# Moving five modulation rows into the up loop, pausing ahead of another, and widening the last batch of the down projection

## The chip, the cores and the metric

The kernel runs on one core of one Trainium2 chip. The metric is the device time of one execution in microseconds (us); lower is better. Engines are named as the profile names them: PE (matmul), PEld (its weight loads), DVE (vector), ACT (activation), POOL (GpSimd), SP (which only issues transfers here).

## The reference

One layer of a diffusion backbone runs over 512 sample tokens and 128 context tokens, all with model width 1024. Its modulation vector is `silu(cvec) @ w_ada + b_ada`, 6144 wide for each of two inputs (`c` and `c_ctx`); split six ways it gives two shifts, two scales and two gains:

```python
mod = jax.nn.silu(cvec) @ lw['w_ada'] + lw['b_ada']
sh1, sc1, g1, sh2, sc2, g2 = jnp.split(mod, 6, axis=-1)
h = rmsnorm(x, lw['norm1_g']) * (1.0 + sc1) + sh1
...                                    # token mixers, gates, w_o
x = x + g1 * mix
h = rmsnorm(x, lw['norm2_g']) * (1.0 + sc2) + sh2
x = x + g2 * conv_ffn(h, lw['w_up'], lw['ffn_conv_w'], lw['ffn_conv_b'], lw['w_down'])
```

`conv_ffn` is an up projection to 2 x 2816 columns, a three-tap convolution over tokens, `silu(g) * a`, and a down projection back to 1024. After the layer both token groups get a final RMS norm with `final_norm_g`. Neighbourhood attention is one of the four mixers.

## The kernel before, in words

**Number format.** Every large product is done three times, as high x high, high x low and low x high parts of float32; the part called "high" is made by a copy on ACT, the part called "low" by a subtraction on DVE or by an accumulating transfer that POOL issues. So each weight block that PE uses costs ACT and DVE work ahead of it ("preparing operands").

**Order.** The program is written out by hand in the order of PE. A small planner (`now`, `tick`, `start`, `step`, L89 to L122) advances a clock by the PE time of each matmul group; side jobs are Python generators that yield how long they want to wait, and they are written into the program when they fall due. A scheduler then orders each engine's instructions by when it believes their inputs to be ready. An instruction wrapped in `keep_in_program_order` (short: `keep_`, `sync` for transfers of SP, `ovec`/`oact`/`opool` inside the up loop) is pinned behind the instruction written last on its engine. Each engine then runs its queue strictly in order: one that waits holds up all behind it.

**Modulation rows.** The 6144 outputs are 48 "rows" of 128 columns. Rows 0 to 15 are done by PE at the start. The others are done on DVE: a 512 KB block of transposed weights is loaded (`H`, `X0`, `A` or `G`), and two `scalar_tensor_tensor` instructions (L285, one per input; the two inputs after silu stand in `S0`) multiply and sum it; a short instruction then writes the result, `modulate` (L231 or L234) for shifts and scales, `gain_col` (L291) for gains. Before the change `ada_cols` (L240) does rows 16 to 41 as a side job while the mixers run, each row yielding 1.4 between its parts and 2.2 ahead of the next; rows 42 to 47 are made inside the down projection by `col_make`, at the units that `COLS` names. Rows 40 to 47 are the gain g2, needed only at the outputs of the down projection, where `gain_rows(1)` (unit 26) and `gain_load` (unit 27) turn them into a broadcast tile in `S0`.

**Attention.** `attn` (L728) is another side job. Its steps for a pair of heads and a block of columns are s1 (scores on PE, sum at L848, maximum at L850, exponential on ACT at L851), s2 (reciprocal L857, scaling L858, transposes on PE at L861, a copy out) and s3 (values on PE at L878). It yields, times 1.1, 4.2 after the first s1, then in each turn 1.5 and 0.6 ahead of s2 and 3.2 behind it.

**Up loop.** `up_pair(p_, r)` (L1614) runs for p_ = 0 to 22. One pair is seven products of 12 matmuls (84 matmuls; a Strassen-like scheme with operands `A`, `B`, `C` and results added in PSUM). In each pair DVE subtracts and adds partial results, applies convolution taps (`taps`), and prepares the next pair's weights (`up_al`, `up_sums`, `up_bl`); ACT does copies, `centre` and silu (`gate`). All of it is pinned.

**Down projection.** 42 units, seven phases of six (`PHASES`, `DOWN`, L1807); a unit is two k steps (the sixth one), and has 12 or 18 matmuls of 512 columns. `ahead` issues the weight loads up to five units and prepares operands up to three units ahead. A unit named in `JOIN` holds its matmuls for the next one: in the last phase units 3, 4 and 5 run as one batch of five k steps, token tile by token tile (t = 0, 1, then 4 in two halves of 256 columns). Behind each token tile stand `half_two` and its parts: `gained` (L1960) and `added` (L1964) on DVE, a square on ACT (L2028), `half_join` (L2045), the root on POOL (`down_root`, L2048), the scaling (`down_scale` on ACT, `down_gain` at L2063 on DVE) and the store. Units named in `LATER` carry finished pieces of earlier phases; `final_gains` multiplies five half tiles by the final norm's weights on POOL and stores tiles 2 and 3.

Of the kernel before, what the change touches and what calls it, by code (L numbers as in the profile page):

```python
# [15 lines left out]

P = 128
HY = 5
AE = (("fb", 1), 0.5, 0.5, 42)
COLWAIT = {}  # L20
HD = [4, 5, 2.1, 7, 2.2, 1.4, 1.5, 5, 2.0, 2, 11]
NPAIR = 22
NK = NPAIR // 2
# [27 lines left out]
D = 1024  # L51
# [19 lines left out]
def tile_step(ctx: ExitStack, tc: tile.TileContext, a: dict, outs: list, dbg=None):  # L71
# [216 lines left out]
        return ar, steps()  # L288

    def gain_col(f, ar):  # L290
        vec.tensor_scalar(gcol[:, f // 8 // 5, :, f % 8], ar, p1[:, C_BADA + f:C_BADA + f + 1], None, ALU.add)  # L291

    def col_home(f):

# [1319 lines left out]
    def up_pair(p_, r):  # L1614


        n, q, o = p_ + 1, p_ - 1, p_ - 2
        inner, nx = p_ < NPAIR, n < NPAIR
        if p_ == 0:
            up_u2(p_)  # L1620
            up_back(1, "C", unit(1, 2), 5, 5, True)
            operand3()
# [10 lines left out]
        if nx and n >= BRIDGE:  # L1633
            up_ah(n, r[n][0])
            up_al(n, r[n][0])
        if inner and p_ >= BRIDGE:
            up_start(p_)
            first_sum(p_)
# [89 lines left out]
    def up_all(_):  # L1728
        fx["x"] = {1: (hh[0][:, 0], hh[0][:, 1]), 2: (hh[0][:, 2], hh[0][:, 3])}
        up_back(2, "A", unit(2, 0), 0, 4)  # L1730
        up_back(3, "A", unit(3, 0), 1, 4)
        up_back(0, "B", unit(0, 1), 2, 5)
        up_back(1, "B", unit(1, 1), 4, 5)
        drain(lambda: "n2_2" in R)
        for p_ in range(BRIDGE):
            up_start(p_)
            if p_ == 1:
                drain(lambda: "n2_3" in R)
                operands(0, 192)
# [12 lines left out]
        col_open()  # L1752

    units.append((lambda: None, lambda pr: None, up_all))


# [18 lines left out]
    def x_load(tag, part=None):  # L1775
# [11 lines left out]
        else:  # L1787
# [2 lines left out]
                xr[h, c] = region(tag, [P, 10, 256])  # L1790
            ks = slice(0, 10) if part is None else slice(5 * part, 5 * part + 5)
            sync(xr[h, c][:, ks], actx[h, c][:, ks])
            if part == 1:
                x_tail(h, c)

    def x_tail(h, c):
# [64 lines left out]
    hold = []  # L1861

    LAST = range(AE[3], 48)
    cols = {}

    def col_open():
        cols["c"] = region("S0", [P, 2, D])
        cf = cols["c"].rearrange("p v c -> p (v c)")
        sync(cf, a["cc"].rearrange("v c -> (v c)").partition_broadcast(P))
        keep_(act(cf, cf, AF.Silu))  # L1870
        for f in LAST[0:2]:
            col_load(f)

    def col_load(f):
        if f in LAST:
            cols[f] = region("HG"[f % 2], [P, D])
            sync(cols[f], a["w_adt"][f - 16])

    def col_make(f):
# [4 lines left out]
            pass  # L1884
        gain_col(f, ar[0])

    COLS = dict(zip((23, 21, 19, 9, 6, 3), range(47, 39, -1)))
    G2 = 27

    def down_start(u):  # L1890
        ph, j = DOWN[u]
        if u == 0:
# [5 lines left out]
        for tag, part in {0: (("A", 0), ("B", 0)), 2: (("A", 1), ("B", 1)), 6: (("D", 0),), 8: (("D", 1),),  # L1898
                          10: (("F", None),)}.get(u, ()):
            x_load(tag, part)  # L1900
        if u == 12:
            x2[2:4] = [x2r("X1")[:, 0:1024], x2r("X1")[:, 1024:2048]]
        if u - 2 in COLS:
            col_load(COLS[u - 2] + 2)
        if u in COLS:
            col_make(COLS[u])
        if u == G2 - 1:
# [16 lines left out]
    def down_tile(u, ws):  # L1924
# [9 lines left out]
        for t in (0, 1, 4) if hp is not None else (0, 1):  # L1934
            halved = p_ == 3 and t == 4 and end
            for ci, (c0, c1) in enumerate(((0, 256), (256, 512)) if halved else ((0, 512),)):
# [76 lines left out]
    def out_22(t):  # L2013
        joined(1, t + 2, acc["b2"][t], acc["u3"][t], ALU.subtract)

    LATER = {(5, 1): (lambda: out_22(0),), (5, 3): (lambda: out_22(1),), (5, 5): (lambda: out_11(0),),
             (6, 1): (lambda: out_11(1),), (6, 2): (lambda: out_11(4),), (6, 3): (final_gains,)}

    def half_two(nh, t, c0, c1, ps):
        xs = x2[t][:, nh * 512 + c0:nh * 512 + c1]  # L2020
        q1, q2 = (st3[:, i + t:i + t + 1] for i in (8, 16))
        keep_(gained(nh, t, c0, c1, ps))
        if t == 4 and c0 == 0:
            half_join(1, 8)
            down_root(1)
        keep_(added(nh, t, c0, c1))
        if c0 == 0:
            keep_(act(prods[t], xs, AF.Square, accum_out=q1))  # L2028
        if t == 1:
            down_store(nh, 0)  # L2030
        elif t < 4:
            half_join(t, 8)
            down_root(t)
        elif c0 > 0:
            half_join(t, 8)
            down_scale(nh, 1)
            keep_(vec.scalar_tensor_tensor(prods[t], xs, 1.0, xs, ALU.mult, ALU.mult, accum_out=q2))
            half_join(t, 16)
            down_root(t)
            down_gain(nh, 1)  # L2040
            down_store(nh, t)

    def half_join(t, i):
# [367 lines left out]
```

## Time and profile before

| | us |
|---|---|
| median of 3 runs | 1016.45 (1016.23 to 1018.08) |
| profiled execution, its time | 1015.32 |
| profiled execution, span of its instructions | 1013.2 |
| PE busy in it | 993.9 |
| DVE busy | 823.8 |
| ACT busy | 559.4 |
| mean granted PE clock | 0.996 |

The span is counted from the first to the last instruction of the profiled execution. In a timeline row the first number is the start in us from the span's start, the second the duration, then engine, line, operation, output and inputs, shape, count; in brackets the idle time of that engine just before it and what ended it. In a window row each engine has its busy time and, in brackets, its instruction count; then the granted PE clock as a share of full speed, the busy share of the transfer engines, and GB/s. "issue" is time with no wait that the profile shows. A line number can be that of a helper: L151 is the pinned form used in the up loop.

### The profile page before, as it was taken

Reading aid. Unit: us, or ns where it says so; the run is one execution under the profiler, and the core shown is the slowest. Engines: PE = TensorE matmul, PEld = TensorE weight load, DVE = VectorE, ACT = ScalarE, POOL = GpSimd, SP = SyncE. Lnnn points to the kernel's source line nnn. Section 1 sums busy time; section 2 is a strip of 40 time slices with the busy share of each in tenths; the row PEclk is TensorE's granted clock in tenths of the full one; section 3 lists DMA queues with packets and bytes.
Section 4 is the critical chain, followed back from the end, with each engine's and each line's share of the span. In section 5 each row is a group of like instructions: output and inputs, shape, how many; then the busy total and the mean of one; then the engine's idle time right before and its main releaser. Section 6 shows DMA issues by size and latency. Waiting matters only on the chain. (4 is left out here: it accounts for less than half of the span.)

```text
span 1013.2 us, 18951 instructions
## 1 busy us (share of the span) xinstructions
PE 993.9 (98%) x7503; PEld 941.4 (93%) x7503; DVE 823.8 (81%) x1381; ACT 559.4 (55%) x983; POOL 168.6 (17%) x223
## 2 busy tenths in 40 slices
PE   8999999997999999999999999999999999999996
PEld 6899999997999999999998899999999999888885
DVE  6778899867775667677778778998888887999897
ACT  6642343343464445444445376777777777756563
POOL 1000020322220122241010021222222222100013
PEclk9999999999999999999999999999999999999999
DMA  9875344596576399799249774766555666996462
GB/s 355 327 255 162 104 148 126 146 265 198 130 216 242 120 276 184 271 281 209 94 145 338 306 267 139 198 169 151 152 151 151 156 155 186 378 353 234 158 247 104
DMA packets 70010, 208.93 MB, mean 206 GB/s; under 512 B 9633, under 2 KB 24769, under 8 KB 67233
## 3 DMA queue, kind: packets, MB, share of 16 engines
q1 hardware_dynamic: 43536, 148.60, 41.2%
q0 software_dynamic: 26384, 59.12, 25.5%
q8 instruction: 59, 0.97, 0.4%
q14 instruction: 31, 0.25, 0.1%
HBM read 165.99 MB, written 48.51 MB: 212 GB/s over the span
## 5 line engine op out<-in xcount | busy, mean ns | idle before, releaser
L375 PE MATMUL g<-XH,w 128*128 128x320 f32 x704 | 171.7, 318 | 0.1
L375 PEld LDWEIGHTS g<-XH,w 128*128 128x128 f32 x704 | 121.2, 189 | 2.7 <-issue 1.0
L375 PE MATMUL g<-XL,w 128*128 128x320 f32 x352 | 109.0, 310 | 0.0
L375 PEld LDWEIGHTS g<-XL,w 128*128 128x128 f32 x352 | 66.6, 189 | 0.0
L1943 PE MATMUL m<-w,XH 128*128 128x512 f32 x246 | 58.6, 390 | 0.0
L1943 PEld LDWEIGHTS m<-w,XH 128*128 128x128 f32 x246 | 46.1, 188 | 9.7
L1152 PE MATMUL m<-XH,w 128*128 128x320 f32 x224 | 52.5, 309 | 0.0
L151 POOL DMA_DIRECT2D wsum<-in_w_dn_dram x36 | 36.5, 1154 | 53.0 <-issue 41.7
L151 ACT ACTIVATE w<-raw 128x1024 fp32r<-128x1024 f32 (+3 forms) x46 | 38.5, 852 | 2.3 <-DMA raw<-in_w_in_dram 1.1
L151 DVE SCALAR_TENSOR_TENSOR X<-MG,p2t,X 128x641 f32<-128x641 f32 x44 | 38.9, 884 | 1.1 <-ACT X L151 0.2
L151 DVE SCALAR_TENSOR_TENSOR X<-X,p2t,X 128x641 f32<-128x641 f32 x44 | 38.9, 884 | 1.0
L1512 PE MATMUL g<-XL,w 128*128 128x320 f32 x240 | 38.7, 310 | 0.0
L1152 PEld LDWEIGHTS m<-XH,w 128*128 128x128 f32 x224 | 38.3, 188 | 0.0
L1512 PE MATMUL g<-XL,C 128*128 128x320 f32 x240 | 38.3, 309 | 0.0
L1512 PEld LDWEIGHTS g<-XL,w 128*128 128x128 f32 x240 | 36.0, 188 | 0.6 <-ACT MG L151 0.3
L1512 PEld LDWEIGHTS g<-XL,C 128*128 128x128 f32 x240 | 36.0, 188 | 0.0
L1152 PE MATMUL m<-XL,w 128*128 128x320 f32 x112 | 34.6, 309 | 0.0
L151 ACT ACTIVATE ga<-m,cst 128x320 f32<-128x320 f32 x27 | 14.3, 528 | 36.6 <-PE m L1152 36.6
L151 DVE TENSOR_TENSOR w<-raw,w 128x1024 fp32r<-128x1024 f32 (+2 forms) x36 | 30.6, 871 | 2.5 <-ACT w L151 2.5
L151 ACT ACTIVATE X<-g 128x320 f32<-128x320 f32 x30 | 13.1, 437 | 34.6 <-PE g L1512 34.5
L1858 DVE TENSOR_TENSOR w<-raw,w 128x1024 fp32r<-128x1024 f32 (+1 forms) x26 | 30.1, 1156 | 2.5 <-ACT w L1854 2.5
L151 DVE TENSOR_TENSOR gb<-g,gb 128x640 f32<-128x640 f32 x12 | 9.9, 825 | 26.3 <-PE g L1165 25.4
(582 smaller groups left out, 2929.8 us busy)
## 6 DMA issues: line engine op xcount, KB each, us to landing
wsum<-in_w_dn_dram POOLq DMA_DIRECT2D x30, 512.0 KB, 11.7
raw<-in_w_up_dram SPq DMA_DIRECT2D x30, 512.0 KB, 5.5
raw<-in_w_gp_dram SPq DMA_DIRECT2D x21, 640.0 KB, 6.6
raw<-in_w_in_dram SPq DMA_DIRECT2D x19, 512.0 KB, 4.5
H<-in_w_adt_dram SPq DMA_DIRECT2D x16, 512.0 KB, 4.5
raw<-wsum SPq DMA_DIRECT2D x12, 512.0 KB, 5.3
actx<-X POOLq DMA_DIRECT2D x22, 256.0 KB, 4.4
wsum<-wsum POOLq DMA_DIRECT2D x10, 512.0 KB, 11.1
```

What stands on the lines that cost most here:

```text
L151: r = f(*args, **kw)
L375: mm(o, w[:, h, k0 + k, :], r(k)[:, s], start=(k == 0 and i == 0), stop=(k == kt - 1 and i == 2))
L1152: mm(o, w[:, k, :], x[:, k, :], start=(first and k == 0 and j == 0), stop=(k == 3 and j == 2), skip_group_check=True)
L1512: z = mm(o, w[:, k, :], x[:, k, :], start=(first and k == 0 and j == 0), stop=(k == 3 and j == 2), skip_group_check=True)
L1858: vec.tensor_tensor(w[:, 1, 0:n], raw, w[:, 0, 0:n].bitcast(F32), ALU.subtract)
L1943: mm(ps, s[t // 4][:, hx, k, o:o + P], w[:, hw, k, c0:c1], start=first, stop=i == 2 and bi == len(batch) - 1 and k == len(ks) - 1, skip_gr ...
```

## The change

Four things are edited together.

1. `ada_cols` does rows 16 to 39 only, and yields 8 ahead of row 39 (`AE`, `COLWAIT`).
2. Rows 40 to 44 are made in the up loop by the new `up_row`: pairs 6, 9, 12, 15 and 18 write a row's first product, the pair after each its second product, the gain column and the load of the next row. The two inputs are loaded and row 40's weights with them at pair 4 (`col_open`), and their silu is written at pair 6. Only rows 45, 46 and 47 stay in the down projection, at the same units as before (19, 21, 23); rows 46 and 47 are loaded two units ahead.
3. Loads in the down projection come later: `D` at units 9 and 11 (before 6 and 8), `F` at 13 (10), `X1` at 16 (12), the tail for `B` at unit 5 (2).
4. The last batch of the last phase has units 2 to 5, seven k steps instead of five. With it, the subtraction for the context tile moves from unit 2 to unit 1, `final_gains` from unit 3 to unit 5, and the token tiles close differently: tile 0 is scaled and stored right behind its own root, tile 1's root follows its own square, and tile 1 is scaled and stored whole between the two halves of tile 4.

```diff
-AE = (("fb", 1), 0.5, 0.5, 42)
-COLWAIT = {}
+AE = (("fb", 1), 0.5, 0.5, 40)
+COLWAIT = {39: 8}
...
+        if p_ == BRIDGE:
+            col_open()
...
         if nx and n >= BRIDGE:
             up_ah(n, r[n][0])
             up_al(n, r[n][0])
+            up_row(p_)
...
-            if part == 1:
+            if part == 1 and tag != "B":
                 x_tail(h, c)
...
-    JOIN = {(4, 4), (5, 0), (6, 3), (6, 4)}
+    JOIN = {(4, 4), (5, 0), (6, 2), (6, 3), (6, 4)}
...
+    UPROWS = dict(zip((6, 9, 12, 15, 18), LAST))
     cols = {}
+
+    def up_row(p_):
+        if p_ in UPROWS:
+            f = UPROWS[p_]
+            if f == LAST[0]:
+                cf = cols["c"].rearrange("p v c -> p (v c)")
+                keep_(act(cf, cf, AF.Silu))
+            cols["job"] = (f,) + col_products(f, cols.pop(f), cols["c"])
+        if "job" in cols:
+            f, ar, steps = cols["job"]
+            if next(steps) == 1:
+                keep_(gain_col(f, ar))
+                del cols["job"]
+                if f + 1 in LAST:
+                    col_load(f + 1)
...
-        keep_(act(cf, cf, AF.Silu))
-        for f in LAST[0:2]:
-            col_load(f)
+        col_load(LAST[0])
...
-            cols[f] = region("HG"[f % 2], [P, D])
+            cols[f] = region("G" if f == 46 else "H", [P, D])
...
-    COLS = dict(zip((23, 21, 19, 9, 6, 3), range(47, 39, -1)))
+    COLS = dict(zip((23, 21, 19), range(47, 44, -1)))
...
-        if p_ == 3 and j == 2:
+        if p_ == 3 and j == 1:
...
-             (6, 1): (lambda: out_11(1),), (6, 2): (lambda: out_11(4),), (6, 3): (final_gains,)}
+             (6, 1): (lambda: out_11(1),), (6, 2): (lambda: out_11(4),), (6, 5): (final_gains,)}
...
         keep_(gained(nh, t, c0, c1, ps))
-        if t == 4 and c0 == 0:
-            half_join(1, 8)
-            down_root(1)
         keep_(added(nh, t, c0, c1))
         if c0 == 0:
             keep_(act(prods[t], xs, AF.Square, accum_out=q1))
-        if t == 1:
-            down_store(nh, 0)
-        elif t < 4:
+        elif t == 4:
+            half_join(t, 8)
+        if t < 4:
             half_join(t, 8)
             down_root(t)
-        elif c0 > 0:
-            half_join(t, 8)
-            down_scale(nh, 1)
+            if t == 0:
+                down_store(nh, t)
+        elif c0 == 0:
+            down_store(nh, 1)
+        else:
             keep_(vec.scalar_tensor_tensor(prods[t], xs, 1.0, xs, ALU.mult, ALU.mult, accum_out=q2))
             half_join(t, 16)
             down_root(t)
-            down_gain(nh, 1)
             down_store(nh, t)
```

More of the change, by code (lines that the diff above doesn't have):

```diff
@@ L290, in gain_col @@
     def gain_col(f, ar):
-        vec.tensor_scalar(gcol[:, f // 8 // 5, :, f % 8], ar, p1[:, C_BADA + f:C_BADA + f + 1], None, ALU.add)
+        return vec.tensor_scalar(gcol[:, f // 8 // 5, :, f % 8], ar, p1[:, C_BADA + f:C_BADA + f + 1], None, ALU.add)
     def col_home(f):
@@ L1751, in up_all @@
         keep(NPAIR - 1)
-        col_open()
     units.append((lambda: None, lambda pr: None, up_all))
@@ L1897, in down_start @@
             acc["c1"], acc["u2"], acc["cp"] = [r[:, 0], r[:, 1]], [r[:, 2], r[:, 3]], r[:, 4]
-        for tag, part in {0: (("A", 0), ("B", 0)), 2: (("A", 1), ("B", 1)), 6: (("D", 0),), 8: (("D", 1),),
-                          10: (("F", None),)}.get(u, ()):
+        for tag, part in {0: (("A", 0), ("B", 0)), 2: (("A", 1), ("B", 1)), 9: (("D", 0),), 11: (("D", 1),),
+                          13: (("F", None),)}.get(u, ()):
             x_load(tag, part)
-        if u == 12:
+        if u == 5:
+            x_tail(1, 1)
+        if u == 16:
             x2[2:4] = [x2r("X1")[:, 0:1024], x2r("X1")[:, 1024:2048]]
-        if u - 2 in COLS:
-            col_load(COLS[u - 2] + 2)
+        if u + 2 in COLS and COLS[u + 2] > 45:
+            col_load(COLS[u + 2])
         if u in COLS:
```

## The prediction, made before the result was known

> **What bounds the kernel now.** I read the page's busy times and slices first, then the windows, then the one long wait of PE, then the end.
>
> ```profile
> span 1013.2 us, 18951 instructions
> ...
> PE 993.9 (98%) x7503; PEld 941.4 (93%) x7503; DVE 823.8 (81%) x1381; ACT 559.4 (55%) x983; POOL 168.6 (17%) x223
> ...
> PE   8999999997999999999999999999999999999996
> ```
>
> PE is busy 993.9 of 1013.2 us, so at most 19.3 us can be won without removing matmuls. The windows show where they lie:
>
> ```profile
> 225.00:250.00 25.00, 19.27 (x144) 17.61 (x143) 16.70 (x42) 9.14 (x21) 5.18 (x7) 0.93 0.72 229
> ...
> 725.00:750.00 25.00, 25.00 (x173) 25.00 (x172) 22.20 (x34) 17.88 (x31) 6.70 (x10) 1.00 0.60 154
> ...
> 900.00:925.00 25.00, 25.00 (x112) 20.69 (x111) 25.00 (x44) 13.66 (x21) 0.00 (x0) 1.00 0.91 337
> ...
> 1000.00:1025.00 25.00, 4.87 (x36) 4.47 (x34) 8.06 (x19) 3.91 (x9) 2.26 (x3) 0.86 0.26 103
> ```
>
> The reader is to see two holes that this change can touch: 25.00 - 19.27 = 5.73 us in the attention stage, and the end, where PE stops 4.87 us into the last window and 8.3 us of other work follow. In the up loop (725 to 750) and the down projection (900 to 925) PE is full. There DVE work moved away gains nothing by itself, and DVE work added costs nothing until a PE input is late.
>
> **The hole.** These are rows of DVE, PE, SP and ACT around it.
>
> ```profile
> 232.53 1.23 DVE L285 SCALAR_TENSOR_TENSOR junk<-A,S 128x1024 bf16<-128x1024 f32 x1 [7.56 <-DMA A<-in_w_adt_dram]
> ...
> 233.88 0.75 DVE L858 TENSOR_SCALAR X<-X,ast 128x384 f32<-128x384 f32 x2
> ```
> ```profile
> 234.44 1.51 PE L861 MATMUL m<-cst,X 128*128 128x128 f32 x6 [5.73 <-DVE X L858]
> ```
> ```profile
> 221.75 1.96 SPq L251 DMA_DIRECT2D A<-in_w_adt_dram  x1
> ```
> ```profile
> 225.53 0.19 ACT L851 ACTIVATION_READ_ACCUMULATOR X<-X,ast 128x1 f32 x1
> ```
> ```profile
> 234.00:236.00 2.00, 1.56 (x7) 1.59 (x8) 2.00 (x6) 0.00 (x0) 0.83 (x2) 0.50 0.04 15
> 236.00:238.00 2.00, 2.00 (x11) 2.00 (x11) 2.00 (x5) 1.95 (x5) 0.58 (x1) 0.71 0.00 0
> 238.00:240.00 2.00, 2.00 (x20) 1.81 (x20) 2.00 (x8) 0.68 (x2) 0.89 (x1) 1.00 0.66 162
> ```
>
> The L285 here is row 39's first product: it is the odd row in `A`, and after it only rows 40 and 41 follow. Its weights, issued at 221.75, landed at 232.5. DVE stood in front of it for 7.56 us with the softmax scaling (L858) queued behind, although the exponentials were done at 225.72. PE needed L858's output at 234.44 - 5.73 = 228.71. So the chain is: a late transfer, DVE's order, PE. The hole has a second cost, the clock behind it: 1.56 us at 0.50 and 2.00 us at 0.71 lose 0.78 + 0.58 = 1.36 us. Together 7.09 us.
>
> The Trainium skill ("TensorE: Matmul & The Clock Gate", Part 1) says that an idle window of about 3.4 us halves the PE clock, and that about 3.4 us of sustained work restores it. The trace agrees (5.73 us idle, then 0.50, then full by 238). An estimate from that page's figures alone would put the clock's share at up to 1.7 us and the hole at 7.4 instead of 7.09.
>
> **The change part by part.**
>
> *Pause ahead of row 39.* The product is due 8 later. By the planner's yields it was due 1.4 + 2.2 = 3.6 behind row 38's second product, just ahead of the second s1; now it is due 11.6 behind it. Row 38's second product is written at about the first s1, so s3 and the third s1, due 1.1 x (4.2 + 1.5 + 0.6 + 3.2) = 10.45 behind that, come first, and the product is pinned behind their DVE work. That work cannot start before about 228.71 + 3.5 = 232.2 and takes about two L848 and two L850, so the product is reached at 234 or later, when its weights have landed even at the old 232.5. L858 can then run at 225.8, two us ahead of need. Gain 5.73 + 1.36 = 7.09. Bounds: nothing gained if the transfer slips as far again, all 7.09 if it lands by 234; I take 7.09, since rows 40 and 41 no longer load behind it. Row 39's own result must be there for the last of four evacuations in this row, which drains until row 39 is done:
>
> ```profile
> L436 DVE TENSOR_TENSOR MG<-g,MG x4: 810/816/824, 245.1 to 278.2; 128x640 f32<-128x640 f32 x4
> ```
>
> At 278.2 - 7.1 = 271 against a row 39 finished near 240 it costs nothing.
>
> *Five rows in the up loop.* Prices, and one pair of the loop (DVE, then PE, then ACT):
>
> ```profile
> L285 DVE SCALAR_TENSOR_TENSOR H<-H,S x16: 1207/1218/1300, 64.7 to 942.1; 128x1024 f32<-128x1024 f32 x16
> L285 DVE DVE_READ_ACCUMULATOR H<-H,S x16: 73/82/85, 65.8 to 943.3; 128x1 f32 x16
> ```
> ```profile
> L291 DVE TENSOR_SCALAR gcol<-ar,cst x16: 210/222/228, 67.0 to 951.3; 128x2 f32<-128x2 f32 x16
> ```
> ```profile
> L1870 ACT ACTIVATE S<-S x1: 1904/1904/1904, 878.0 to 878.0; 128x2048 f32<-128x2048 f32 x1
> ```
> ```profile
> 719.44 1.23 DVE L151 TENSOR_TENSOR w<-raw,w 128x1024 fp32r<-128x1024 f32 x1 [0.35 <-ACT w L151]
> 721.61 0.49 DVE L151 TENSOR_TENSOR MG<-m,s 128x320 f32<-128x320 f32 x1 [0.95 <-PE m L1512]
> ...
> 727.01 0.48 DVE L151 TENSOR_TENSOR X<-g,X 128x320 f32<-128x320 f32 x1
> ```
> ```profile
> 717.82 1.92 PE L1512 MATMUL g<-XH,MG 128*128 128x320 f32 x12
> ...
> 723.10 1.92 PE L1512 MATMUL g<-A,E 128*128 128x320 f32 x12
> ...
> 730.14 1.92 PE L1512 MATMUL g<-XH,w 128*128 128x320 f32 x12
> ```
> ```profile
> 719.78 0.44 ACT L151 ACTIVATE s<-g 128x320 f32<-128x320 f32 x1 [0.38 <-PE g L1512]
> ```
>
> Ten products of 1.22 + 0.08 are 13.0 us and five gain columns 1.1: 14.1 us of DVE over pairs 6 to 19. A pair lasts 730.14 - 717.82 = 12.32 us and DVE idles 0.35 + 0.95 = 1.30 in it, 14 x 1.30 = 18.2 in all. The product is written between the weight subtraction (719.44) and the sum (721.61), exactly in the 0.95 wait. The first product overruns it by 0.35, the second with its gain column by 0.57; the backlog stays under 1 us, and the third pair clears it. What is late next is DVE's subtraction at 727.01, which frees the bank that PE writes from 730.14: 730.14 - 727.49 = 2.65 us of slack, more than the backlog. The silu (1.90, pair 6 only) delays ACT's copy from 719.78 + 0.44 = 720.22 to about 722.1; PE's product that overwrites its source starts at 723.10. Cost on PE: 0, the cover being these 2.65 and 1.0 us; if it were gone, all 14.1 + 1.9 would be the other end. The load of the next row stands on SP behind the second product and ahead of a later pair's weights; an SP that waits 1 us there delays loads whose buffers come free later anyway: 0.
>
> *Rows out of the down projection.* 3 x (2 x 1.30 + 0.22) = 8.5 us less DVE work around 885 to 908, and the silu. PE is full there: 0. *Later loads of D, F, X1, rows 46 and 47:* 0 if they land in time. The nearest row for one that does not is the 5.73 above; I keep 0, since three row loads and that of the inputs leave the same stretch of SP's queue.
>
> *The last batch.* PE, DVE and POOL at the end:
>
> ```profile
> 990.24 2.88 PE L1943 MATMUL m<-MG,XH 128*128 128x512 f32 x12
> ...
> 994.32 1.52 PE L1943 MATMUL m<-A,XH 128*128 128x512 f32 x6
> ...
> 1003.63 1.24 PE L1943 MATMUL m<-w,MG 128*128 128x256 f32 x9
> ```
> ```profile
> 992.67 0.68 DVE L1858 TENSOR_TENSOR w<-raw,w 128x512 fp32r<-128x512 f32 x1
> ...
> 999.59 0.68 DVE L1984 TENSOR_TENSOR y<-m,XL 128x512 f32<-128x512 f32 x1
> ...
> 1001.03 0.69 DVE L1964 TENSOR_TENSOR X<-X,dt 128x512 f32<-128x512 f32 x1
> 1002.58 0.16 DVE L2045 SCALAR_TENSOR_TENSOR st<-st 128x1 f32<-128x1 f32 x1 [0.85 <-ACT dt L2028]
> ...
> 1004.71 0.74 DVE L2063 SCALAR_TENSOR_TENSOR X<-X,st,F 128x512 f32<-128x512 f32 x1
> ...
> 1006.16 0.42 DVE L1960 TENSOR_TENSOR dt<-m,S 128x256 f32<-128x256 f32 x1
> ...
> 1008.80 0.75 DVE L2063 SCALAR_TENSOR_TENSOR G<-G,st,F 128x512 f32<-128x512 f32 x1 [0.44 <-POOL st L2048]
> ```
> ```profile
> 1002.81 0.55 POOL L2048 TENSOR_TENSOR st<-st,neghalf 128x1 f32<-128x1 f32 x1 [5.74 <-DVE st L2045]
> ...
> 1007.78 0.99 POOL L2048 TENSOR_TENSOR st<-st,neghalf 128x1 f32<-128x1 f32 x1 [1.13 <-DVE st L2045]
> ```
>
> A 512-wide matmul takes 2.72/12 = 0.227 us (990.24 to 992.96 in steps of 12). Tile 0 was finished at 994.32 + 15 x 0.227 = 997.7, and will be at 990.24 + 21 x 0.227 = 995.0. But DVE took it up only at 999.59: it is late, not PE, and stays so at the very end (the last half's sum runs at 1006.16, PE ended at 1004.87). The work ahead of 999.59 is the same after the change, so the 2.7 us earlier result is not used. What is new is on DVE's pinned order behind tile 0 (1001.72): it waits for tile 0's root, from 1002.72 to 1002.81 + 0.55 and a start, about 0.73; it waits for tile 1's square, 0.85 as at 1002.58, a wait that other work covered before; and tile 1's scaling, which filled the wait for the last root, now stands ahead of the last half: 0.66. Against it, the last root meets an idle DVE: 0.55 instead of 0.99, 0.44 less. Sum 0.73 + 0.85 + 0.66 - 0.44 = +1.8 us; with a root of 0.99 again, +2.2.
>
> The Trainium skill ("SBUF — State Buffer", "SBUF: two separate sides") says that a DVE instruction with two SBUF inputs and a POOL instruction that reads SBUF exclude each other for their whole length. The trace agrees as far as it goes: the root took 0.55 beside an idle DVE and 0.99 beside DVE's scaling. By that rule the tail costs 1.8, not 2.2.
>
> The operands of the last unit are ready at 992.67 + 0.68 = 993.35 and will be wanted at 990.24 + 18 x 0.227 = 994.3. The context tile's three instructions, now written ahead of them, can make them about 1 us late; that stalls PE, not DVE. Bounds of the tail: -1.2, if DVE is not late at all and the end hangs on PE (1004.87 + (1008.80 - 1006.16) = 1007.5 for the last scaling, with 0.1 for the start, against 1008.80); +3.1, if the last root is no faster and the 0.85 wait comes twice. I take +1.8, nearest to the rows.
>
> **Sum.** -5.73 - 1.36 + 1.8 = -5.3 us. The profiled execution took 1015.32, 1.13 under the median, so it would take 1010.0; from the median 1016.45 I predict 1011.2.
>
> **The rivals.**
> 1. *The up loop becomes DVE's* (slower). DVE is at 22.20 of 25, and the added rows bring it to about 1.00 in two pairs of three. If PE's banks wait behind DVE, up to 14.1 us come back: 1011.2 + 14.1 = 1025.3. It decides once more than 5.3 of the 14.1 reach PE. Against it: the 2.65 us of slack and the third pair. Chance 0.11.
> 2. *The pause does not do it*: the product still meets its transfer ahead of L858, or another row blocks in its place. Then only the tail is left, 1016.45 + 1.8 = 1018.3, or about 1014.7 with half the hole. For it: the scheduler, not the trace, orders the queue. Chance 0.15.
> 3. *The end hangs on PE, not on DVE*: 1016.45 - 7.1 - 1.2 = 1008.2. For it: 2.7 us earlier tiles; against it: DVE saturated up to 999.59. Chance 0.14.
>
> **How the numbers follow.** My forecast has 0.60, around 1009.9 (tail +0.5) to 1012.5 (+3.1). The range reaches over rival 3 with 1 us to spare, and up into rival 2: 1007.2 to 1016.9. A measurement tells about 0.2%, 2 us, from no change. Faster: 0.60, 0.14 and a third of rival 2, less a little for the unknown loads, 0.76; same: the rest of rival 2 and weak forms of rival 1, 0.11; slower: 0.13.
>
> **What would show it.** Right: no L285 with a transfer behind it near 225 to 240, PE full in 225 to 250 at clock 1.00; 84 matmuls in every 12.32 us between pairs 6 and 19; a span from the last matmul to the last scaling longer by 1 to 3 us, with a DVE wait on POOL behind tile 0. Wrong: PE waits in the up loop that are ended by DVE, a new DMA wait in front of DVE anywhere, or PE stalls beyond 1 us in the last batch.

## The result, and the profile after

The changed kernel takes 1012.70 us (median of five executions, 1011.25 to 1013.39) against 1016.45 for the kernel before: a ratio of 0.9957 with a 95% interval of 0.9943 to 0.9972. It is faster by 3.75 us; 5.3 were forecast, and the time lies in the predicted range, 1.5 us above the predicted 1011.2. The profiled execution took 1011.57 us, also 3.75 less than the one before.

Three points carry the comparison, in the profiled executions: the start of the up loop (its first L1512 matmul), the start of unit 2 of the last phase of the down projection (its first matmul), and the start of the last scaling on DVE. In the changed kernel unit 2 opens the last batch; in the kernel before it stands just ahead of the batch of units 3 to 5. So both ways are measured over the same work. The expectations below call this point the last batch's first matmul.

| us | before | after | difference |
|---|---|---|---|
| start to up loop | 610.75 | 603.71 | -7.04 |
| up loop to unit 2 of the last phase | 379.49 | 379.69 | +0.20 |
| unit 2 to last scaling | 18.56 | 21.57 | +3.01 |
| span | 1013.2 | 1009.4 | -3.8 |

So 7.04 us were won in the attention stage and 3.01 were given back at the end. The windows of the changed kernel, the same four as in the prediction (busy us and instruction count of PE, PEld, DVE, ACT and POOL, then granted clock, share of the transfer engines, GB/s):

```profile
225.00:250.00 25.00, 25.00 (x202) 23.03 (x201) 19.46 (x51) 12.40 (x29) 7.42 (x11) 1.00 0.75 230
725.00:750.00 25.00, 25.00 (x173) 25.00 (x172) 23.25 (x35) 17.86 (x31) 6.17 (x8) 1.00 0.62 162
900.00:925.00 25.00, 25.00 (x112) 20.68 (x112) 18.96 (x26) 16.00 (x26) 0.00 (x0) 1.00 0.78 271
1000.00:1025.00 25.00, 0.00 (x0) 0.00 (x0) 4.11 (x12) 2.57 (x6) 1.10 (x2) 0.82 0.13 50
```

The first row is full where 19.27 stood, and its clock is 1.00 where 0.93 stood. The second shows PE still full in the up loop, with DVE at 23.25 instead of 22.20. The last has no matmul any more: what is left there is work of DVE and ACT and two short instructions of POOL.

DVE's timeline of the changed kernel around the former hole (start, duration, engine, line, operation, output and inputs; idle time and its releaser in brackets):

```profile
226.07 0.42 DVE L858 TENSOR_SCALAR X<-X,ast 128x384 f32<-128x384 f32 x1
226.53 1.02 DVE L848 TENSOR_TENSOR X<-m,B 128x384 f32<-128x384 f32 x2
...
234.32 1.02 DVE L848 TENSOR_TENSOR X<-m,B 128x384 f32<-128x384 f32 x2 [0.31 <-PE m L844]
235.26 1.00 DVE L850 TENSOR_REDUCE ast<-X 128x1 f32<-128x384 f32 x2
236.18 1.29 DVE L285 SCALAR_TENSOR_TENSOR junk<-A,S 128x1024 bf16<-128x1024 f32 x1
```

Row 39's first product (L285) now stands behind two further groups of sums, and it waits for nothing: its transfer has landed by then. The scalings (L858) ahead of it run at 225.5 and 226.1.

The sum `MG<-m,s` in three pairs of the up loop, on DVE, with the row products of the first two:

```profile
701.23 1.22 DVE L285 SCALAR_TENSOR_TENSOR junk<-H,S 128x1024 bf16<-128x1024 f32 x1
...
702.37 0.49 DVE L151 TENSOR_TENSOR MG<-m,s 128x320 f32<-128x320 f32 x1
...
713.55 1.22 DVE L285 SCALAR_TENSOR_TENSOR H<-H,S 128x1024 f32<-128x1024 f32 x1
...
714.95 0.48 DVE L151 TENSOR_TENSOR MG<-m,s 128x320 f32<-128x320 f32 x1
...
726.90 0.49 DVE L151 TENSOR_TENSOR MG<-m,s 128x320 f32<-128x320 f32 x1 [0.94 <-PE m L1512]
```

The products fill the place of the wait in front of the sum. In the two pairs with a product that wait is gone; in the third it is back at 0.94, so the backlog is cleared before the next row. Counted back from there in pairs of 12.32 us, the sums of the first two are 0.11 and 0.37 us late.

The end of the changed kernel, on DVE:

```profile
987.12 1.58 DVE L1977 TENSOR_TENSOR dt<-y,S 128x512 f32<-128x512 f32 x1
...
991.43 2.48 DVE L2078 SCALAR_TENSOR_TENSOR X<-X,st,F 128x512 f32<-128x512 f32 x2
993.84 0.68 DVE L2001 TENSOR_TENSOR y<-m,XL 128x512 f32<-128x512 f32 x1
...
995.27 0.69 DVE L1981 TENSOR_TENSOR X<-X,dt 128x512 f32<-128x512 f32 x1
996.75 0.16 DVE L2060 SCALAR_TENSOR_TENSOR st<-st 128x1 f32<-128x1 f32 x1 [0.79 <-ACT dt L2042]
997.58 0.75 DVE L2078 SCALAR_TENSOR_TENSOR X<-X,st,F 128x512 f32<-128x512 f32 x1 [0.66 <-POOL st L2063]
...
1001.23 0.16 DVE L2060 SCALAR_TENSOR_TENSOR st<-st 128x1 f32<-128x1 f32 x1 [0.85 <-ACT dt L2042]
...
1004.97 0.75 DVE L2078 SCALAR_TENSOR_TENSOR G<-G,st,F 128x512 f32<-128x512 f32 x1 [0.66 <-POOL st L2063]
```

On POOL, with the two final gains (L2007) that now come late, and on PE, the first matmuls of unit 2 and the last ones of all:

```profile
986.87 1.28 POOL L2007 TENSOR_TENSOR X<-X,F 128x512 f32<-128x512 f32 x1
991.40 1.30 POOL L2007 TENSOR_TENSOR G<-G,F 128x512 f32<-128x512 f32 x1 [3.25 <-ACT dt L1986]
...
1004.38 0.55 POOL L2063 TENSOR_TENSOR st<-st,neghalf 128x1 f32<-128x1 f32 x1 [2.37 <-DVE st L2060]
```
```profile
983.40 1.52 PE L1960 MATMUL m<-MG,XH 128*128 128x512 f32 x6
...
996.87 1.24 PE L1960 MATMUL m<-w,MG 128*128 128x256 f32 x9
```

Split at the end of tile 0's addition (L1964 before, L1981 after), the 3.01 are two sums. Behind it the way to the last scaling took 1008.80 - 1001.72 = 7.08 us and takes 1004.97 - 995.96 = 9.01: +1.93. DVE's waits there are 0.79, 0.66, 0.85 and 0.66, together 2.96, where they were 0.85 and 0.44; that is 1.67 of it, and the rest, 0.26, lies in short gaps between instructions that need each other's results. Ahead of it, from the first matmul of unit 2, 1001.72 - 990.24 = 11.48 became 995.96 - 983.40 = 12.56: +1.08. There a multiplication by the gain (L1977) took 1.58 us beside one of POOL's final gains, and the two scalings of earlier tiles 2.48 beside the other.

In the kernel before, the same two final gains stood elsewhere. DVE's rows there, and POOL's second one:

```profile
995.59 0.68 DVE L1950 TENSOR_TENSOR y<-g,XL 128x512 f32<-128x512 f32 x1
996.31 1.31 DVE L1960 TENSOR_TENSOR dt<-y,S 128x512 f32<-128x512 f32 x1
```
```profile
995.78 1.29 POOL L1990 TENSOR_TENSOR G<-G,F 128x512 f32<-128x512 f32 x1
```

POOL's first one (994.33 to 995.82) fell into a wait of DVE. The second ran beside the subtraction `y<-g,XL`, which has one operand in PSUM and took its usual 0.68, and then beside the multiplication by the gain, which took 1.31.

### The profile page after: what moved, and what is told of

It is laid out like the page before. It is cut to its first block, busy times and chain, and to the rows that moved or that the text cites. A ratio compares the mean times of both kernels' runs of the same rounds, so it can differ in the third digit from the quotient of the medians.

```text
span 1009.4 us, 18972 instructions
## 1 busy us (share of the span) xinstructions
PE 993.0 (98%) x7509; PEld 940.8 (93%) x7509; DVE 826.7 (82%) x1381; ACT 558.3 (55%) x983; POOL 166.5 (16%) x223
## 5 line engine op out<-in xcount | busy, mean ns | idle before, releaser
L1512 PE MATMUL g<-XL,w 128*128 128x320 f32 x240 | 38.7, 310 | 0.0
L1512 PE MATMUL g<-XL,C 128*128 128x320 f32 x240 | 38.3, 309 | 0.0
L1512 PEld LDWEIGHTS g<-XL,w 128*128 128x128 f32 x240 | 35.9, 188 | 0.7 <-ACT MG L151 0.3
L1512 PEld LDWEIGHTS g<-XL,C 128*128 128x128 f32 x240 | 36.0, 188 | 0.0
L336 ACT ACTIVATE w<-raw 128x1024 fp32r<-128x1024 f32 (+1 forms) x22 | 24.3, 1104 | 12.1 <-PE m L947 8.2
```

Source lines behind the costliest of these rows:

```text
L336: high = lambda: act(w[:, 0], raw, AF.Copy)
L1512: z = mm(o, w[:, k, :], x[:, k, :], start=(first and k == 0 and j == 0), stop=(k == 3 and j == 2), skip_group_check=True)
```

## The experiments

Times are medians; the ratios are to the kernel before on the same chip, with their 95% intervals. "End" is the time from the first matmul of unit 2 of the last phase to the last scaling.

| kernel | time | ratio | end |
|---|---|---|---|
| changed, again | 1012.82 | 0.9959 (0.9946 to 0.9971) | 21.56 |
| old end | 1008.60 | 0.9918 (0.9905 to 0.9932) | 18.58 |
| no pause | 1019.73 | 1.0028 (1.0017 to 1.0040) | 21.60 |
| pause alone | 1009.88 | 0.9934 (0.9922 to 0.9947) | 18.58 |
| new end alone | 1019.67 | 1.0029 (1.0018 to 1.0041) | 21.61 |
| new batch, old closing order | 1010.13 | 0.9930 (0.9917 to 0.9942) | 19.62 |
| two final gains left out | 1009.66 | 0.9925 (0.9913 to 0.9938) | 19.64 |
| old end, products twice | 1012.72 | 0.9956 (0.9941 to 0.9971) | 18.57 |
| old end, joins later | 1007.96 | 0.9907 (0.9894 to 0.9921) | 17.63 |
| old end, pause of 4 | 1016.02 | 0.9996 (0.9986 to 1.0005) | 18.60 |

### The old end

```diff
-    JOIN = {(4, 4), (5, 0), (6, 2), (6, 3), (6, 4)}
+    JOIN = {(4, 4), (5, 0), (6, 3), (6, 4)}
...
-        if p_ == 3 and j == 1:
+        if p_ == 3 and j == 2:
...
-             (6, 1): (lambda: out_11(1),), (6, 2): (lambda: out_11(4),), (6, 5): (final_gains,)}
+             (6, 1): (lambda: out_11(1),), (6, 2): (lambda: out_11(4),), (6, 3): (final_gains,)}
...
         keep_(gained(nh, t, c0, c1, ps))
+        if t == 4 and c0 == 0:
+            half_join(1, 8)
+            down_root(1)
         keep_(added(nh, t, c0, c1))
...
-        if t < 4:
+        if t == 1:
+            down_store(nh, 0)
+        elif t < 4:
             half_join(t, 8)
             down_root(t)
-            if t == 0:
-                down_store(nh, t)
-        elif c0 == 0:
-            down_store(nh, 1)
...
+            down_gain(nh, 1)
             down_store(nh, t)
```

> The changed kernel with its last batch undone: units 3 to 5 as one batch of five k steps, the old closing order of the token tiles, the context tile's subtraction at unit 2 and the final gains at unit 3. Theory A (the hole in the attention stage is the whole gain, about 7 us; the new end costs what the two traces differ by, 21.57 - 18.56 = 3.0 us from the last batch's first matmul to the last scaling): about 1012.7 - 3.0 = 1009.7 us, and 18.5 us from the first matmul of the last batch to the last scaling. Rival B (the new end is neutral or gains, and the gap between 7 and 3.7 lies elsewhere, in the rows moved to the up loop or the later loads): 1012.7 or more.

It took 1008.60 us, 8.25 less than the kernel before and 4.1 less than the changed one. Its end, on PE and on DVE:

```profile
983.43 2.88 PE L1960 MATMUL m<-MG,XH 128*128 128x512 f32 x12
```
```profile
1002.01 0.75 DVE L2080 SCALAR_TENSOR_TENSOR G<-G,st,F 128x512 f32<-128x512 f32 x1 [0.44 <-POOL st L2065]
```

Theory A holds. Both kernels start unit 2 of the last phase at 983.4, and this one is at the last scaling 2.96 us sooner (1002.01 against 1004.97). The new end is a plain loss; the profiled executions differ by 3.02 us, which it accounts for. The medians differ by 4.1, and the other 1.1 isn't explained: the profiled execution of the changed kernel is one of its fastest. From the start of the up loop to unit 2 this kernel takes 983.43 - 603.94 = 379.49 us, the same as the kernel before.

### The new end alone

This is the kernel before with the three edits shown here and the new `half_two`, and nothing else:

```diff
-    JOIN = {(4, 4), (5, 0), (6, 3), (6, 4)}
+    JOIN = {(4, 4), (5, 0), (6, 2), (6, 3), (6, 4)}
...
-        if p_ == 3 and j == 2:
+        if p_ == 3 and j == 1:
...
-             (6, 1): (lambda: out_11(1),), (6, 2): (lambda: out_11(4),), (6, 3): (final_gains,)}
+             (6, 1): (lambda: out_11(1),), (6, 2): (lambda: out_11(4),), (6, 5): (final_gains,)}
...
```

> The kernel before with the new last batch alone: units 2 to 5 as one batch of seven k steps, the context tile's subtraction at unit 1, the final gains at unit 5, the new closing order. Theory A (the new end costs 3.0 us: 1.9 by the closing order, 1.1 by the final gains on POOL running beside DVE's scalings): 1016.45 + 3.0 = 1019.4 us. The prediction's own step: + 1.8, 1018.3. Rival B (the new end gains because tile 0 is ready 2.7 us earlier): 1016.45 - 1.2 = 1015.2 us or less.

It is slower, 1019.67 us: 2.82 above the kernel before, as theory A has it, and its end takes 1014.34 - 992.73 = 21.61 us. The same end costs the same three microseconds with and without the rest of the change.

### No pause

```diff
-COLWAIT = {39: 8}
+COLWAIT = {}
```

> The changed kernel without the pause ahead of row 39; rows 40 and 41 stay in the up loop. Theory A (the pause moves row 39's first product behind the next heads' sums and maxima, and this alone closes the hole): the hole is back, PE busy about 19.3 of 25 us between 225 and 250 at a clock near 0.93, and the time is 1012.7 + 7.1 = 1019.8 us. Rival B (rows 40 and 41 no longer load behind row 39, so its weights come early enough without a pause): about 1012.7, no wait of DVE on row 39's transfer ahead of the softmax scaling.

It took 1019.73 us, 7.0 above the changed kernel. The hole is back, as theory A says. It also equals the kernel with the new end alone (1019.67), from which it differs only by the rows moved and the later loads: without the pause these two together are worth nothing that the times show. DVE's wait, PE's wait, and the clock behind it:

```profile
232.79 1.23 DVE L285 SCALAR_TENSOR_TENSOR junk<-A,S 128x1024 bf16<-128x1024 f32 x1 [7.87 <-DMA A<-in_w_adt_dram]
```
```profile
234.70 1.51 PE L861 MATMUL m<-cst,X 128*128 128x128 f32 x6 [6.05 <-DVE X L858]
```
```profile
234.00:236.00 2.00, 1.30 (x7) 1.33 (x7) 2.00 (x9) 0.00 (x0) 0.57 (x1) 0.50 0.01 3
236.00:238.00 2.00, 2.00 (x9) 2.00 (x9) 2.00 (x5) 1.70 (x5) 0.84 (x2) 0.50 0.00 0
238.00:240.00 2.00, 2.00 (x10) 2.00 (x9) 1.45 (x6) 0.93 (x2) 0.89 (x1) 0.56 0.00 0
```

Rows 40 and 41 were already gone here, and the transfer still landed at 232.8: it isn't they that make it late. The clock stayed near half until 240, where it was full by 238 in the profile of the kernel before. PE was busy 1.30, 2.00 and 2.00 us at 0.50, 0.50 and 0.56: that loses 0.65 + 1.00 + 0.88 = 2.5 us instead of 1.36. So nearly the same hole costs 7.1 us in one execution and about 6.05 + 2.5 = 8.6 in another.

### The pause alone

```diff
-COLWAIT = {}
+COLWAIT = {39: 8}
```

That is made in the kernel before; rows 40 to 47 stay where they were.

> The kernel before with the pause ahead of row 39 alone; rows 40 and 41 still follow it among the mixers, and 42 to 47 stay in the down projection. Theory A (the pause alone closes the hole): 1016.45 - 7.1 = 1009.4 us, PE full between 225 and 250. Rival B (rows 40 and 41, pushed later by 8, block DVE or the last evacuations of the attention stage in row 39's place): a new idle stretch of PE between 240 and 290 that is ended by DVE or a transfer, and 1014 to 1018 us.

It took 1009.88 us, 6.97 less than the kernel before. Theory A holds in the main (1009.4 expected), and rival B in part: a delay has come behind it, but a far smaller one than its 1014 to 1018 us. Two windows, and PE's wait:

```profile
252.00:258.00 6.00, 5.92 (x49) 5.33 (x49) 6.00 (x15) 0.86 (x4) 0.20 (x1) 1.00 0.74 165
258.00:264.00 6.00, 5.66 (x41) 4.45 (x39) 4.34 (x14) 4.01 (x7) 2.33 (x3) 1.00 0.32 109
```
```profile
260.62 0.94 PE L861 MATMUL m<-cst,X 128*128 128x128 f32 x6 [0.34 <-DVE X L858]
```

DVE is busy without a gap from 252 to 258, behind and with the products of row 41 (250.67 to 254.23), and the up loop starts at 605.28, where it starts at 603.94 in the kernel with the rows moved and the old end. So taking rows 40 and 41 out of the mixers is worth 1.3 us once the pause pushes them to a later place; the medians of the two kernels differ by the same 1.3 (1009.88 and 1008.60). Only 0.08 + 0.34 us of that shows as idle time of PE; where the rest goes, its rows don't tell.

### A pause of 4

```diff
-COLWAIT = {39: 8}
+COLWAIT = {39: 4}
```

That is made in the kernel with the old end.

> The kernel with the rows moved, the pause and the old last batch (1008.6 us), but with a pause of 4 instead of 8: row 39's first product is now written right behind the softmax scaling that PE waits for, and ahead of the next heads' sums. Theory A (all that the pause has to do is to bring the product behind that scaling; the next sums are needed only some 4 us later, when the weights have landed): no hole, 1008.6 us. Rival B (the product must also stand behind the next sums and maxima, as the prediction had it): DVE waits for the weights in front of those sums, PE stands 1 to 3 us between 230 and 240, and 1010 to 1013 us.

My expectation fell. It took 1016.02 us, no faster than the kernel before. DVE and PE:

```profile
226.02 0.42 DVE L858 TENSOR_SCALAR X<-X,ast 128x384 f32<-128x384 f32 x1
232.19 1.23 DVE L285 SCALAR_TENSOR_TENSOR junk<-A,S 128x1024 bf16<-128x1024 f32 x1 [5.75 <-DMA A<-in_w_adt_dram]
...
233.34 1.02 DVE L848 TENSOR_TENSOR X<-m,B 128x384 f32<-128x384 f32 x2
```
```profile
236.99 1.44 PE L878 MATMUL m<-B,X 128*64 128x128 f32 x7 [4.49 <-DVE B L2137]
```

The product now stands behind the scaling (L858) that PE had waited for. But the next sums (L848), which ran at 226.53 in the changed kernel, are queued behind it and start at 233.34. PE comes to stand 4.49 us at another line. Rival B has the mechanism, but not the price: it had 1 to 3 us of standing PE and 1010 to 1013 us. The clock behind the stand (granted 0.50 from 236 to 240 and 0.66 from 240 to 242, with PE busy 1.01, 2.00 and 2.00 us) loses about 2.2 us more, and a wait of 0.76 us in the down projection brings the sum to the 7.4 us between this kernel and the one with a pause of 8. It isn't enough to bring the product that waits for the late transfer behind the next thing that PE needs: it has to go behind everything that is needed until the transfer lands.

### The new batch with the old closing order

The changed kernel takes back the edit of `half_two` alone:

```diff
         keep_(gained(nh, t, c0, c1, ps))
+        if t == 4 and c0 == 0:
+            half_join(1, 8)
+            down_root(1)
         keep_(added(nh, t, c0, c1))
...
-            if t == 0:
-                down_store(nh, t)
-        elif c0 == 0:
-            down_store(nh, 1)
...
```

> The changed kernel with the batch of seven k steps, the subtraction at unit 1 and the final gains at unit 5 kept, but with the closing order of the token tiles as before: tile 0 is stored behind tile 1's square, tile 1's root and scaling stand among the halves of tile 4. Theory A (of the 3.0 us that the new end costs, the closing order is 1.9, by two waits for a root or a square and a scaling that stands ahead of the last half; the later final gains are 1.1): from the last batch's first matmul to the last scaling 21.57 - 1.9 = 19.7 us, and 1008.6 + 1.1 = 1009.7 us. Rival B (the waits cost nothing, since a DVE held up by the batch or the gains would be late anyway): 21.5 us and about 1012.

The end takes 1003.72 - 984.10 = 19.62 us, 1.95 less than in the changed kernel: theory A, to 0.1. What stays of the +3.0 is 19.62 - 18.58 = 1.04, and it lies ahead of the end of tile 0's addition, which comes 12.60 us after unit 2 has begun (11.48 before). The time is 1010.13, 0.4 more than expected; PE lost 0.87 us ahead of the batch:

```profile
971.94 2.81 PE L1960 MATMUL m<-A,XH 128*128 128x512 f32 x11 [0.87 <-DVE A L1859]
```

### Two final gains left out

```diff
         for nh, t in ((1, 2), (1, 3), (0, 0), (0, 1), (0, 4)):
-            final_gain(nh, t)
+            if (nh, t) not in ((0, 1), (0, 4)):
+                final_gain(nh, t)
```

> The changed kernel without two of POOL's five final gains: the first halves of tile 1 and of the context tile are not multiplied by the final norm's weights, so those two half tiles leave unscaled by them; all else is the changed kernel. Theory A (DVE's instructions with two operands beside these POOL multiplications take longer: one 1.58 instead of 0.68, a pair of scalings 2.48 instead of 1.41): DVE reaches tile 0 some 0.90 + 1.07 = 2.0 us earlier, 21.57 - 2.0 = 19.6 us from the last batch's first matmul to the last scaling, and 1012.7 - 2.0 = 1010.7 us. Rival B (the long instructions waited for something else): both times as in the changed kernel, 21.6 and 1012.7.

The same DVE instructions, without POOL's multiplications beside them:

```profile
986.64 0.69 DVE L1977 TENSOR_TENSOR dt<-y,S 128x512 f32<-128x512 f32 x1
...
990.06 1.41 DVE L2079 SCALAR_TENSOR_TENSOR X<-X,st,F 128x512 f32<-128x512 f32 x2
...
1002.52 0.75 DVE L2079 SCALAR_TENSOR_TENSOR G<-G,st,F 128x512 f32<-128x512 f32 x1 [0.66 <-POOL st L2064]
```

Theory A holds: 0.69 instead of 1.58 and 1.41 instead of 2.48, and an end of 1002.52 - 982.88 = 19.64 us, 1.93 less. The medians differ by more, 3.0 us (1012.70 and 1009.66); the profiled executions by 2.44 (1011.57 and 1009.13), of which 0.52 lies ahead of unit 2. So up to 1.1 of the 3.0 isn't explained by the end.

### The products twice

```diff
             for v in range(2):
+                if twice:
+                    tc.keep_in_program_order(
+                        vec.scalar_tensor_tensor(junk, raw, 1.0, cr[:, 0], ALU.mult, ALU.mult, accum_out=ar[:, 0:1]))
                 tc.keep_in_program_order(
```

That is made in the kernel with the old end, and `twice` is set for the rows of the up loop alone.

> The kernel with the rows moved, the pause and the old last batch (1008.6 us), but with the first product of each row written once more in each of the ten pairs that have one: 10 x 1.30 = 13 us more DVE work in the up loop, which changes no result. Theory A (the five rows cost nothing because they fit into the 1.30 us that DVE idles in a pair; twice as much does not): a row's three pairs now ask for 4 x 1.30 + 0.22 = 5.4 us of 3.9 idle, 1.5 too many, five rows 7.6, of which 2.65 are absorbed by the slack in front of PE: 1008.6 + 5 to 8 = 1013.6 to 1016.6 us, with waits of PE in the up loop that are ended by DVE. Rival B (DVE had more room than the idle time of one pair shows): 1008.6 to 1010.

It took 1012.72 us, 4.1 more, a little less than theory A's 5 to 8. Unit 2 of the last phase starts at 987.47 instead of 983.43, so all of it is lost ahead of the end. Fifty microseconds of the up loop:

```profile
700.00:750.00 50.00, 49.77 (x338) 49.30 (x337) 49.47 (x77) 34.36 (x60) 12.32 (x16) 1.00 0.64 166
```

DVE is busy 49.47 of 50 us, and PE issues 338 matmuls there against 343 in the kernel with single products. So 13 us more bring DVE to its bound, and the kernel loses 4.

The loss doesn't reach PE in the way that theory A has it. PE's waits in this stretch are put down to ACT, not to DVE, and they are waits of its weight loads. Rows of PE with single products (the kernel with the old end), then with the products twice:

```profile
711.02 1.92 PE L1512 MATMUL g<-XH,MG 128*128 128x320 f32 x12
712.78 1.92 PE L1512 MATMUL m<-XH,MG 128*128 128x320 f32 x12
...
716.30 1.92 PE L1512 MATMUL g<-A,E 128*128 128x320 f32 x12
```
```profile
712.13 1.92 PE L1515 MATMUL g<-XH,MG 128*128 128x320 f32 x12
713.89 0.46 PE L1515 MATMUL m<-XH,MG 128*128 128x320 f32 x2
714.18 0.46 PE L1515 MATMUL m<-XH,w 128*128 128x320 f32 x2
```
```profile
714.58 1.18 PEld L1515 LDWEIGHTS g<-A,E 128*128 128x128 f32 x8 [0.20 <-ACT s L151]
```

The order of PE has changed with the added work. Between `g<-XH,MG`, whose result ACT copies (`s<-g`), and `g<-A,E`, which waits for that copy, there stood 24 matmuls; now there are four. From 640 to 860 the products `m<-XH` stood whole, twelve in a row, 16 times, and do so twice here. The weight loads wait eight times for that copy, 0.20 or 0.50 us each, 2.8 in all; most of the rest are waits for ACT at the passage to the down projection. So this run shows that twice the work no longer fits without loss. It doesn't show how much DVE's time alone would cost, with PE's order kept.

### The joins later

```diff
+        if t == 1:
+            half_join(0, 8)
+            down_root(0)
         keep_(gained(nh, t, c0, c1, ps))
+        if t == 0:
+            q = st3[:, 4:5]
+            keep_(vec.tensor_scalar(q, q, 1.0 / D, EPS, ALU.mult, ALU.add))
...
-        elif t < 4:
+        elif 0 < t < 4:
             half_join(t, 8)
             down_root(t)
```

That is made in the kernel with the old end; the short instruction written here behind tile 0's product is the one that `half_one` no longer writes for the context tile's first half.

> The kernel with the rows moved, the pause and the old last batch (1008.6 us), with two short DVE instructions that wait 0.85 us each on a square of ACT written later: the context tile's first half sum of squares behind tile 0's product with the gain, and tile 0's sum and root behind tile 1's subtraction. Theory A (at the end DVE is late, not PE, so each wait of DVE that is covered by other work comes off the time): DVE comes 1.5 us earlier to the last halves, of which 1.3 remain until it waits for PE itself: 1008.6 - 1.3 = 1007.3 us, 17.3 us from the last batch's first matmul to the last scaling. Rival B (PE holds the end): 1008.6.

The end takes 1001.95 - 984.32 = 17.63 us, 0.95 less of the 1.3 expected: DVE is what holds the end, and most of a wait that other work covers comes off it. The time is 1007.96, only 0.64 less, and the intervals of the two kernels overlap. In the profiled execution PE had lost 0.90 us at the start of the second phase of the down projection:

```profile
888.32 1.65 PE L1960 MATMUL g<-w,MG 128*128 128x512 f32 x6 [0.90 <-ACT XL L1994]
```

It has the lowest time of all kernels here, 9.0 us under the kernel before (1016.95 on that chip).

### The changed kernel again

> The changed kernel itself once more, beside the kernel before on one chip, since its five times were spread over 2.1 us (1011.25 to 1013.39), more than those of the kernel with the old last batch (1008.12 to 1008.77). By the traces it should stand 3.0 us above that kernel: 1011.6. By the medians so far it stands 4.1 above: 1012.7.

1012.82 us (1011.32 to 1013.94) against 1016.64 before: the first result again, and the same spread. Its profiled execution was its fastest, 1011.32. Two more profiles of the same kernel:

> The changed kernel once more, for one profile: both profiled executions so far (1011.57 and 1011.32) were among its fastest, and its others went up to 1013.94. If the spread sits in the new end, a slower execution shows more than 21.6 us from the last batch's first matmul to the last scaling; if it sits ahead of it, the end stays at 21.6 and a wait of PE or a slow clock appears earlier, most likely on the operands of the down projection (0.9 us in two of the other kernels).

> The same once more, with the same two readings: the end at 21.6 us and the rest elsewhere, or a longer end.

They took 1011.71 and 1012.18 us, with ends of 21.61 and 21.60. The spread doesn't sit in the end. In the slower of them PE lost 0.5 us in the down projection, at the place where the kernel with the joins later lost 0.90:

```profile
PE g L1960 <- ACT XL L1993: 0.5, 1, 0.5
```

What makes an execution of 1013.9 was not caught in a profile and stays open.

## Why the prediction was right in sign and 1.5 us off

**The hole, -7.09: right, by its mechanism and its place.** The prediction had the product pinned behind the third s1, reached "at 234 or later", with the scaling at 225.8 and no wait. It was reached at 236.18, with scalings at 225.47 and 226.07, and the up loop started 7.04 us sooner. That this meets 7.09 to 0.05 is partly luck. Both are read against the same profiled execution of the kernel before, and by the medians the pause and the rows with the old end win 8.25. Without the pause the hole was back. With half of it the product is due at 7.6 by the prediction's count, ahead of the 10.45 of the third s1; it came to stand ahead of those sums, and the gain was gone. That "rows 40 and 41 no longer load behind it" was not what mattered for the transfer, which landed at 232.8 without them all the same. It mattered in another way: left among the mixers with the pause, they cost 1.3 us.

The price was one execution's. Its clock part, 1.36, was 2.5 in the profile without the pause, more than the prediction's estimate of up to 1.7. The Trainium skill ("TensorE: Matmul & The Clock Gate", Part 1) says that the clock's activity window runs freely, so that the same kernel spends a different time at half speed, at its start, from run to run. These two profiles agree with that for a hole in the middle, with the clock full by 238 in one and only by 240 in the other, though their holes also differ by 0.32 us. It may be part of why twelve executions of the kernel before spread over 2.6 us (1015.51 to 1018.08); but the changed kernel, which has no hole, spreads as far, so it can't be all.

**Five rows in the up loop, 0: right.** The products used up the wait in front of the sum in two pairs, the third waited 0.94 again, and the way from the up loop to unit 2 of the last phase grew by 0.20; with the old end it is 379.49, as before. The first rival (DVE-bound, 1025.3) did not come. The doubled products show that there was little room left: 13 us more cost 4, though by way of another order of PE.

**Rows out of the down projection and later loads, 0: not refuted.** Both lie within the same 0.00 to 0.20, and the kernel without the pause (1019.73) and the new end alone (1019.67) differ by these and the moved rows together. None of the three was tried alone.

**The tail, +1.8: mis-sized. It was +3.01, near the upper bound of 3.1 but not for that bound's reasons.** The terms behind tile 0 were right as a sum (+1.93 measured): the waits of 0.66 for tile 0's root and 0.85 for tile 1's square came, tile 1's scaling stood ahead of the last half, and the last root took 0.55. (The row at 1006.16, which the prediction calls the last half's sum, is its multiplication by the gain; no term changes by that.) The step that failed is the sentence "The work ahead of 999.59 is the same after the change". It is not. `final_gains` moved from unit 3 to unit 5, and with it two multiplications of POOL slid beside DVE instructions with two operands in SBUF. Before, they ran beside a wait and a subtraction with an operand in PSUM, and slowed one multiplication by the gain (1.31 us at 996.31). Now they slow that multiplication to 1.58 and a pair of scalings to 2.48. By the durations with the gains left out that is 1.58 + 2.48 - 0.69 - 1.41 = 1.96 where it was 1.31 - 0.69 = 0.62: 1.3 more, which covers the +1.08. Leaving the two multiplications out took 1.93 off the end, so they are the cause; that the kernel before paid 0.62 for them is read from its rows and was not tried.

The prediction had the rule for this in hand and used it on the roots alone. The Trainium skill ("SBUF — State Buffer", "SBUF: two separate sides") says that such a DVE instruction and a POOL instruction that reads SBUF lock each other out for the whole instruction. The trace agrees: DVE's instruction of 987.12 ends at 988.70, which is POOL's end (986.87 + 1.28 = 988.15) and then 0.55. In the kernel before, the instruction of 996.31 ends at 997.62, again 0.55 behind POOL's end (995.78 + 1.29 = 997.07), while the subtraction `y<-g,XL`, with one operand in PSUM, kept its 0.68 beside the same instruction of POOL. So the price could be read from the profile before.

**The third rival (the end hangs on PE, 1008.2): refuted.** PE ended at 998.1 and the last scaling came 6.9 us later; earlier tiles were worth nothing, since DVE took up tile 0 at 993.84, 5.6 us after PE had finished it (983.40 + 21 x 0.227 = 988.2). **The second rival (the pause does not do it): refuted** for the change; something like it, a hole at another line, is what a pause of 4 brings. PE did not stall in the last batch.

In the sum: -7.04 + 0.20 + 3.01 = -3.83 against a predicted -5.3, and 1.2 of the 1.5 us between them are the tail's.

## What to carry to other kernels

An instruction that waits for a late transfer has to stand in its engine's queue behind everything that is needed before the transfer lands; behind the one instruction that the trace names as blocked is not enough, and the next one takes its place. When work moves on a second engine, list what will run beside it there: one of DVE's two-operand instructions took 1.58 us instead of 0.69 beside a POOL multiplication. And at the end of this kernel, finishing PE's tiles earlier won nothing, since DVE was the late engine; there DVE's own waits and the lengths of its instructions counted.

## What the runs showed that was not expected

- Nearly one hole, two prices: 5.73 us of idle PE cost 1.36 us of clock behind it, 6.05 us cost 2.5.
- A POOL multiplication of 1.3 us took 0.9 (1.58 against 0.69) and 1.07 us (2.48 against 1.41 for a pair) from DVE, nearly its own length, while an instruction with an operand in PSUM lost nothing (0.68).
- 13 us of work added to a DVE that idles 1.30 us of each pair also changed the order of PE's matmuls, and most of the 4.1 us that it cost show as waits of PE's weight loads for copies of ACT.
